# Recurrence gates: the middle output's neighbour rows as one 96-row stacked product instead of a 128-row and a 64-row one

## Chip, core and metric

The kernel runs on one core of a Trainium2 chip. The metric is device time in microseconds (us) from one launch; lower is better. Three runs of the kernel before took 801.54, 803.41 and 803.30 us.

## What is computed

Two layers of a streaming-encoder trunk over 256 tokens of 1024 channels. Each layer normalises the tokens, projects them by one wide matrix, and feeds three mixers: a spatial gate (A), an attention with eight heads (B), and a gated recurrence (C). Their gated outputs are projected, summed, projected again, normalised and added to the tokens. The change touches mixer C only. There, 1280 channels are convolved along time, and two gates are computed from the result by block-diagonal matrices:

```python
xb = xc.reshape(B, S, LRU_BLOCKS, LRU_BW)          # 16 blocks of 80 channels
r = sigmoid(einsum('bshi,hij->bshj', xb, w_a) + b_a)
i = sigmoid(einsum('bshi,hij->bshj', xb, w_x) + b_x)
log_a = -LRU_C * r * softplus(-lam)
h_t = exp(log_a) * h_{t-1} + sqrt(max(1 - exp(2 * log_a), 0)) * (i * xc)
```

A block has 80 channels, a tile of the machine 128 rows: five tiles hold eight blocks, and some blocks lie across two tiles.

## The kernel before

**Weights.** All weights come from main memory as float32 in chunks of up to 128x2048. A chunk is loaded into one of three `raw` buffers by the SP queue, and split into two float32r parts, one rounded (`hi`, written by ScalarE, ACT) and one that holds what the rounding lost (`lo`, written by VectorE, DVE), in one of three pairs `whi`/`wlo`. A product is three matmuls: hi by hi, hi by lo, lo by hi (`mm3`, lines 307 to 309). When a step has used its chunk, `fin` gives the pair back, and `pump` splits the next chunk into it and starts the load after that. So ACT and DVE run ahead of TensorE (PE) by up to three chunks.

**Order.** The table `ORDER` sets one fixed order of steps in each layer. Every engine works its own instructions in that order, and waits on semaphores where it needs another engine. The steps that matter here are `stack` (`conv_stack`, once for each of two groups of five tiles), `la` and `lx` (`lru_gate`, the two gates, each once for each group). Around them the order is: `ga` 0, `la` 0, `lx` 0, `r1` 0, `stack` 1, `pa` 0, `ga` 1, `pa` 1, `la` 1, `r2` 0, `r3` 0, `ga` 2, `pa` 2, `zb` 0, `ga` 3, `zb` 1, `lx` 1.

**The gate matrices.** Of a group's five output tiles, 1 and 3 take their own tile and two neighbours by two full products of three matmuls each. The outputs 0, 2 and 4 take their own tile by three matmuls, and a few rows of their odd neighbours, which are stacked in one operand `xs`. For outputs 0 and 4 that is one run of 32 rows, laid three times one under the other (hi, lo, hi) against weights laid as (hi, hi, lo): one 96-row matmul does all three passes. Output 2 has two neighbours, and so two runs of 32 rows. Two copies fill 128 rows (hi and lo against hi and hi), and the third pass is a matmul of its own over 64 rows (line 930, from `xs[:64]` and `wlo`):

```python
r = 3 * SH if n < 2 else P
mm3(pm, wh[:, e], wl[:, e], xh[:, m], xl[:, m], True, False)
mm(pm, wh[:r, d], xs[:r, n], start=False, stop=n < 2)
if n == 2:
    mm(pm, wl[: 2 * SH, d], xs[: 2 * SH, n], start=False, stop=True)
```

There are eight calls of `lru_gate` (two gates, two groups, two layers), so there are eight such 64-row matmuls.

**Setting up the rows.** `conv_stack` copies the runs into `xs`; the table `SE` names the engine of each ("G" is GpSimd, POOL; "A" is ACT; "V" is DVE). For the stack of output 2, part 0 goes to POOL, and parts 1 and 2 to ACT; before, part 2 does not exist. `split` lays out the weights: line 259 rounds all 1280 columns, lines 261 and 262 copy the stacked columns to lower rows, lines 263 and 264 form the lo part.

Of the kernel before, what the change touches and what calls it, by code (L numbers as in the profile page):

```python
# [13 lines left out]
P = 128  # L14
# [19 lines left out]
# Rows of the per-layer table of channel vectors, 128 channels each.  # L34
R_Q, R_KV, R_LG, R_LB, R_CW, R_CB, R_BA, R_BX, R_LAM, R_N = 0, 3, 5, 13, 21, 61, 71, 81, 91, 101

# A group of five 128-channel tiles holds eight 80-channel blocks, of which the blocks 1, 3, 4 and 6 lie
# across two tiles. The even input tiles meet all outputs in one strip of columns: their own tile's, and
# between them those of the tiles 1 and 3, which two even tiles share (the lower rows from the one, the
# upper rows from the other). The odd input tiles meet their own output, and a few rows of them those of  # L40
# the tiles 0, 2 and 4: those rows stand in one operand for two or three of the float32r products.
COL_EVEN, COL_ODD, COL_STACK, LRU_N = 0, GT * P, (GT + 2) * P, (GT + 5) * P
# Of a stack: the output, its rows, and their runs of 32: input tile, first row.
STACKS = ((0, 32, ((1, 0),)), (4, 32, ((3, 96),)), (2, 64, ((1, 96), (3, 0))))
# [4 lines left out]
# Order of a layer's steps between the ranks and the output projection.  # L49
# [14 lines left out]
# Of what steps the weights make room for the next ones only after the step's arithmetic, and how late.  # L64
LATE = {"ga": 1, "gb": 1, "lx": 1, "pa": 1, "ukv": 1, "uq": 3, "v": 1, "xc": 1}

# Engines that set out the rows of the stacks.
# [7 lines left out]
class Chunk:  # L75
    """A piece of weights on its way: loaded as float32, then split into two float32r parts."""
# [17 lines left out]
def tile_trunk(ctx: ExitStack, tc, I, out):  # L94
# [24 lines left out]
    def ring(pool, s, n, shape, dt=F32):  # L119
        """n buffers taken in turn."""  # L120
        bufs = [pool.tile(shape, dt, tag=f"{s}{i}", name=f"{s}{i}") for i in range(n)]
        turn = [0]

        def take(_=None):
            turn[0] += 1
            return bufs[(turn[0] - 1) % n]

        return take
# [64 lines left out]
    def load(c, parts=1, mid=None):  # L193
        n = c.kt * c.cols
        c.raw = raw_()
        if c.lru is None:
            raw, src, m = v2(c.raw[:, :n], c.cols), c.src(), c.kt // parts
            for i in range(parts):
                nc.sync.dma_start(raw[:, i * m : (i + 1) * m], src[:, i * m : (i + 1) * m])
                if i == 0 and mid:  # L200
                    mid()
            return
        name, l, g = c.lru
        G.memset(c.raw[:, :n], 0.0)

        def piece(row, col, r0, c0, nr, ncol):
            """A piece of a block of the group, its rows and columns counted from the group's start."""
            b = r0 // BW
            nc.sync.dma_start(
                c.raw[row : row + nr, col : col + ncol],  # L210
                I[name][l, g * 8 + b, r0 - b * BW : r0 - b * BW + nr, c0 - b * BW : c0 - b * BW + ncol],
            )

        for b in range(8):
            for k in range(GT):
                r0, r1 = max(b * BW, k * P), min(b * BW + BW, k * P + P)
                if r0 < r1 and k % 2 == 0:
                    piece(r0 - k * P, COL_EVEN + b * BW, r0, b * BW, r1 - r0, BW)
                elif r0 < r1:
                    c0, c1 = max(b * BW, k * P), min(b * BW + BW, k * P + P)  # L220
                    piece(r0 - k * P, COL_ODD + k // 2 * P + c0 - k * P, r0, c0, r1 - r0, c1 - c0)
        for n_, (m, _, runs) in enumerate(STACKS):
            for i, (k, r) in enumerate(runs):
                for b in range(8):
                    r0, r1 = max(b * BW, k * P + r), min(b * BW + BW, k * P + r + SH)
                    c0, c1 = max(b * BW, m * P), min(b * BW + BW, m * P + P)
                    if r0 < r1 and c0 < c1:
                        piece(i * SH + r0 - k * P - r, COL_STACK + n_ * P + c0 - m * P, r0, c0, r1 - r0, c1 - c0)

    def split(c, parts=1, mid=None):  # L230
# [17 lines left out]
        if c.kind == "heads":  # L248
            # Columns of two heads, set out as their unrotated parts and then their rotated ones.
            raw = c.raw[:, :n].rearrange("p (k h r) -> p k h r", h=2, r=HN + HR)  # L250
            for a, b, o in ((0, HN, 0), (HN, HN + HR, 2 * HN)):
                w = b - a
                src = raw[:, :, :, a:b]
                h4, l4 = (v[:, :, o : o + 2 * w].rearrange("p k (h r) -> p k h r", r=w) for v in (c.hi, c.lo))
                act(h4, src, AF.Copy)
                V.tensor_tensor(l4, src, f(h4), ALU.subtract)
            return
        if c.lru:
            act(hi[:, :n], c.raw[:, :n], AF.Copy)
            one, two = slice(COL_STACK, COL_STACK + 2 * P), slice(COL_STACK + 2 * P, n)  # L260
            act(hi[SH : 2 * SH, one], c.raw[:SH, one], AF.Copy)
            act(hi[2 * SH :, two], c.raw[: 2 * SH, two], AF.Copy)
            V.tensor_tensor(lo[:, :n], c.raw[:, :n], f(hi[:, :n]), ALU.subtract)
            V.tensor_tensor(hi[2 * SH : 3 * SH, one], c.raw[:SH, one], f(hi[:SH, one]), ALU.subtract)
            return
# [12 lines left out]
    def pump(most=3, **how):  # L278
        """Splits the next chunks, as far as there is room for their parts, and loads what follows."""
# [76 lines left out]
    def layer_decay(c):  # L356
        # 8 * softplus(-lambda), with log1p(e) = 2 artanh(e / (2 + e)).
# [30 lines left out]
    def sums(n):  # L388
        """Room for n partial means of squares, and the term that goes with them."""
        ss = small("ssq", n + 1)  # L390
        G.memset(ss[:, n : n + 1], EPS)
        return ss
# [33 lines left out]
    def tok_mm(ps, c, t):  # L426
        """Tokens of tile t on partitions, the chunk's channels along the free axis."""
        for k in range(KT):
            lh, ll = hT[0][:, t, k], hT[1][:, t, k]
            rh, rl = c.h(k, 0, CW), c.l(k, 0, CW)  # L430
            mm(ps, lh, rh, start=k == 0, stop=False)  # L431
            mm(ps, lh, rl, start=False, stop=False)  # L432
            mm(ps, ll, rh, start=False, stop=k == KT - 1)  # L433

    def ch_mm(ps, c, seq=None):
        """Two tiles of channels on partitions, all tokens along the free axis."""
# [18 lines left out]
    # ======================================================================  # L455
    with tc.manual_schedule():
# [19 lines left out]
        # The tensor engine reaches its full clock only when it has been busy for some time.  # L476
# [6 lines left out]
        def first_norm(t):  # L483
            """The first layer's norm and transpose: the tokens' factors by a product with a diagonal."""
# [46 lines left out]
        for l in range(L):  # L531
# [169 lines left out]
            def conv_stack(g):  # L701
                """What the odd outputs take from two even tiles, and the stacks of the even outputs."""
# [5 lines left out]
                for n, (_, nr, runs) in enumerate(STACKS):  # L708
                    for p, src in enumerate((xh, xl, xh)[: P // nr]):
                        for i, (k, r) in enumerate(runs):  # L710
                            at = p * nr + i * SH
                            copy(SE.get(("thin", n, p), "V"), xs[at : at + SH, n], f(src[r : r + SH, k]))
# [61 lines left out]
            def attend(i):  # L774
                """The i-th pair of heads' scores, and what follows for the pairs before."""
# [103 lines left out]
            def gated(key, src, n):  # L879
                """Adds a gated projection's channels to the sum."""  # L880
# [24 lines left out]
            hs, gates = {}, {}  # L905

            def lru_gate(key, row):
                def step(g):
# [4 lines left out]
                    for m0 in range(0, GT, 2):  # L913
                        ms = range(m0, min(m0 + 2, GT))
                        ps = bank() if len(ms) == 2 else aux()
                        for m in ms:
# [6 lines left out]
                            else:  # L923
                                n = (0, 4, 2).index(m)
                                d = slice(COL_STACK + n * P, COL_STACK + n * P + P)
                                r = 3 * SH if n < 2 else P
                                mm3(pm, wh[:, e], wl[:, e], xh[:, m], xl[:, m], True, False)
                                mm(pm, wh[:r, d], xs[:r, n], start=False, stop=n < 2)
                                if n == 2:
                                    mm(pm, wl[: 2 * SH, d], xs[: 2 * SH, n], start=False, stop=True)  # L930
# [20 lines left out]
            def recur2(g):  # L951
                # 1 - a^2 = tanh(-log a) (1 + a^2)
# [163 lines left out]
```

## Time and profile before

| | us |
|---|---|
| runs | 801.54, 803.41, 803.30; median 803.3 |
| span of the profiled execution, first to last instruction | 799.7 |
| PE busy, share of the span | 790.8, 99% |
| DVE busy | 551.3, 69% |
| ACT busy | 468.1, 59% |
| POOL busy | 68.9, 9% |

The profile gives the profiled execution's own time as its span only: 799.7 us. The median of the runs lies 3.6 us above it, which is what stands around the span (and what differs between executions). "PE" is the matmul side of TensorE, "PEld" its weight loads. A timeline row gives the start, the duration, the engine, the line in the code, the operation, output<-inputs, and the shape. A matmul's duration (0.28 us) is longer than the distance to the next one, since matmuls overlap in a pipeline; what one costs a full stream is the distance between two starts. Under 800 us, 0.3% is 2.4 us.

### The profile page before, as it was taken

The page shows a single profiled execution, that of the slowest core. Times are in us where ns is not written, and L with a number is a line of the kernel's source. Part 1 is how long each engine was busy: PE and PEld are TensorE (multiplying, and loading weights), DVE is VectorE, ACT ScalarE, POOL GpSimd, SP SyncE. Part 2 cuts the span into 40 slices and gives each one's busy share as a digit, 9 for nine tenths or more (in the row PEclk, how much of TensorE's full clock was granted, in tenths as well). Part 3 has the DMA queues.
Part 4 walks back from the last instruction along what each step waited for, and adds up shares of the span by engine and source line. Part 5 has one row for each costly group of instructions (what it writes and reads, how often), then busy time and mean ns, then how long its engine had stood idle before and what let it go on. Part 6 is the DMA issues. An engine that isn't in the chain of part 4 may idle for free.

```text
span 799.7 us, 15378 instructions
## 1 busy us (share of the span) xinstructions
PE 790.8 (99%) x6453; PEld 780.9 (98%) x6453; DVE 551.3 (69%) x712; ACT 468.1 (59%) x689; POOL 68.9 (9%) x110
## 2 busy tenths in 40 slices
PE   8999999999999999999999999999999999999996
PEld 8999999999999999999999999999999999999996
DVE  5686788567776787555666868776578578775562
ACT  5785766349755736343567776754695574544441
POOL 1100503103000000000010032031210000000000
PEclk9999999999999999999999999999999999999999
DMA  7855454344566465566357626541575656564531
GB/s 235 284 167 183 151 164 131 114 136 151 170 212 211 158 214 170 197 213 216 106 171 242 212 86 210 158 144 34 167 222 161 212 163 207 185 210 149 195 132 53
DMA packets 134205, 137.87 MB, mean 172 GB/s; under 512 B 11046, under 2 KB 130808, under 8 KB 134136
## 3 DMA queue, kind: packets, MB, share of 16 engines
q1 hardware_dynamic: 134120, 136.90, 54.1%
q8 instruction: 50, 0.82, 0.4%
q14 instruction: 19, 0.16, 0.1%
q10 hardware_dynamic: 16, 0.00, 0.0%
HBM read 135.83 MB, written 1.05 MB: 171 GB/s over the span
## 4 chain that ended last, share of the span: by engine, by line
PE 96%; issue 1%; DMA 1%; DVE 0%; ACT 0%; SPq 0%; POOL 0%; POOLq 0%; DVEq 0%
PE mm L307 25%; PE mm L308 25%; PE mm L309 24%; PE mm L431 2%; PE mm L432 2%; PE mm L433 2%; PE mm L549 1%; PE mm L547 1%; PE mm L548 1%; PE aux L843 1%; PE aux L770 1%; PE mm L730 1%; PE mm L731 1%; DMA X<-in_x_dram 1%; PE aux L1024 1%
## 5 line engine op out<-in xcount | busy, mean ns | idle before, releaser
L269 DVE TENSOR_TENSOR wlo<-raw,whi 128x2048 fp32r<-128x2048 f32 (+5 forms) x123 | 264.7, 2157 | 117.0 <-ACT whi L268 116.6
L307 PE MATMUL mm<-hT,whi 128*128 128x256 f32 x1088 | 307.4, 283 | 0.0
L309 PE MATMUL mm<-hT,wlo 128*128 128x256 f32 x1088 | 306.0, 281 | 0.0
L308 PE MATMUL mm<-hT,whi 128*128 128x256 f32 x1088 | 305.9, 281 | 0.0
L268 ACT ACTIVATE whi<-raw 128x2048 fp32r<-128x2048 f32 (+5 forms) x123 | 220.9, 1802 | 68.8 <-PE mm L308 27.8
L308 PEld LDWEIGHTS mm<-hT,whi 128*128 128x128 f32 x1088 | 205.3, 189 | 0.0
L309 PEld LDWEIGHTS mm<-hT,wlo 128*128 128x128 f32 x1088 | 205.2, 189 | 0.1
L307 PEld LDWEIGHTS mm<-hT,whi 128*128 128x128 f32 x1088 | 205.2, 189 | 0.0
L976 ACT ACTIVATE t<-mm 128x512 f32<-128x512 f32 x18 | 10.8, 598 | 53.4 <-PE mm L309 53.4
L397 POOL TENSOR_TENSOR rstd<-rstd,mhalf 128x1 f32<-128x1 f32 x8 | 4.4, 549 | 392.9 <-DVE rstd L396 392.9
L308 PE MATMUL mm<-yc,whi 128*128 128x256 f32 x128 | 36.1, 282 | 0.0
L308 PE MATMUL mm<-ya,whi 128*128 128x256 f32 x128 | 36.1, 282 | 0.0
L307 PE MATMUL mm<-ya,whi 128*128 128x256 f32 x128 | 36.0, 281 | 0.0
L307 PE MATMUL mm<-yc,whi 128*128 128x256 f32 x128 | 36.0, 281 | 0.0
L431 PE MATMUL mm<-whi,hT 128*128 128x256 f32 x128 | 36.0, 281 | 0.0
L309 PE MATMUL mm<-ya,wlo 128*128 128x256 f32 x128 | 35.9, 281 | 0.0
L308 PE MATMUL mm<-yb,whi 128*128 128x256 f32 x128 | 35.9, 281 | 0.0
L309 PE MATMUL mm<-yc,wlo 128*128 128x256 f32 x128 | 35.9, 280 | 0.0
L309 PE MATMUL mm<-yb,wlo 128*128 128x256 f32 x128 | 35.8, 280 | 0.0
L307 PE MATMUL mm<-yb,whi 128*128 128x256 f32 x128 | 35.8, 280 | 0.0
L432 PE MATMUL mm<-wlo,hT 128*128 128x256 f32 x128 | 35.8, 280 | 0.0
L433 PE MATMUL mm<-whi,hT 128*128 128x256 f32 x128 | 35.7, 279 | 0.0
(281 smaller groups left out, 1666.4 us busy)
## 6 DMA issues: line engine op xcount, KB each, us to landing
raw<-in_w_in_dram SPq DMA_DIRECT2D x76, 1024.0 KB
raw<-in_w_proj_a_dram SPq DMA_DIRECT2D x8, 1024.0 KB
raw<-in_w_proj_b_dram SPq DMA_DIRECT2D x8, 1024.0 KB
raw<-in_w_proj_c_dram SPq DMA_DIRECT2D x8, 1024.0 KB
raw<-in_w_out_dram SPq DMA_DIRECT2D x8, 1024.0 KB
raw<-in_mla_w_uq_dram SPq DMA_DIRECT2D x8, 576.0 KB
raw<-in_mla_w_ukv_dram SPq DMA_DIRECT2D x4, 1024.0 KB
raw<-in_w_in_dram SPq DMA_DIRECT2D x4, 640.0 KB
```

The costliest lines, as they stand in the source:

```text
L268: act(hi[:, w], c.raw[:, w], AF.Copy)
L269: V.tensor_tensor(lo[:, w], c.raw[:, w], f(hi[:, w]), ALU.subtract)
L307: mm(ps, lh, rh, start=start, stop=False)
L308: mm(ps, lh, rl, start=False, stop=False)
L309: mm(ps, ll, rh, start=False, stop=stop)
L431: mm(ps, lh, rh, start=k == 0, stop=False)
L432: mm(ps, lh, rl, start=False, stop=False)
L433: mm(ps, ll, rh, start=False, stop=k == KT - 1)
L547: mm(ps, lh, rh, start=j % 2 + k == 0, stop=False)
L548: mm(ps, lh, rl, start=False, stop=False)
L549: mm(ps, ll, rh, start=False, stop=j % 2 * 4 + k == KT - 1)
L976: act(sg, ps, AF.Sigmoid)
```

## The change

The two runs of output 2 overlap in need only by 16 rows each: of tile 1 the rows 112 to 127, of tile 3 the rows 0 to 15. After, both stand in one run of 32: 32 rows of tile 1 from row 96 are copied first, and then 16 rows of tile 3 over the first 16 of them. So output 2 has the same shape as outputs 0 and 4: three parts of 32 rows, one 96-row matmul, and no 64-row one. The copies become 32 and 16 rows for each of three parts, where they were 32 and 32 for each of two. The weights' split treats all three stacks alike: one copy of 32x384 on ACT in place of 32x256 and 64x128, and a lo part of 896 columns in place of 1280. The number of DMAs does not change.

```diff
-STACKS = ((0, 32, ((1, 0),)), (4, 32, ((3, 96),)), (2, 64, ((1, 96), (3, 0))))
+STACKS = ((0, ((1, 0, 32),)), (4, ((3, 96, 32),)), (2, ((1, 96, 32), (3, 0, 16))))
...
-                    r0, r1 = max(b * BW, k * P + r), min(b * BW + BW, k * P + r + SH)
+                    r0, r1 = max(b * BW, k * P + r), min(b * BW + BW, k * P + r + nr)
...
-                        piece(i * SH + r0 - k * P - r, COL_STACK + n_ * P + c0 - m * P, r0, c0, r1 - r0, c1 - c0)
+                        piece(r0 - k * P - r, COL_STACK + n_ * P + c0 - m * P, r0, c0, r1 - r0, c1 - c0)
...
             act(hi[:, :n], c.raw[:, :n], AF.Copy)
-            one, two = slice(COL_STACK, COL_STACK + 2 * P), slice(COL_STACK + 2 * P, n)
-            act(hi[SH : 2 * SH, one], c.raw[:SH, one], AF.Copy)
-            act(hi[2 * SH :, two], c.raw[: 2 * SH, two], AF.Copy)
-            V.tensor_tensor(lo[:, :n], c.raw[:, :n], f(hi[:, :n]), ALU.subtract)
-            V.tensor_tensor(hi[2 * SH : 3 * SH, one], c.raw[:SH, one], f(hi[:SH, one]), ALU.subtract)
+            st = slice(COL_STACK, n)
+            act(hi[SH : 2 * SH, st], c.raw[:SH, st], AF.Copy)
+            V.tensor_tensor(lo[:, :COL_STACK], c.raw[:, :COL_STACK], f(hi[:, :COL_STACK]), ALU.subtract)
+            V.tensor_tensor(hi[2 * SH : 3 * SH, st], c.raw[:SH, st], f(hi[:SH, st]), ALU.subtract)
...
-                for n, (_, nr, runs) in enumerate(STACKS):
-                    for p, src in enumerate((xh, xl, xh)[: P // nr]):
-                        for i, (k, r) in enumerate(runs):
-                            at = p * nr + i * SH
-                            copy(SE.get(("thin", n, p), "V"), xs[at : at + SH, n], f(src[r : r + SH, k]))
+                for n, (_, runs) in enumerate(STACKS):
+                    for p, src in enumerate((xh, xl, xh)):
+                        at = p * SH
+                        for k, r, nr in runs:
+                            copy(SE.get(("thin", n, p), "V"), xs[at : at + nr, n], f(src[r : r + nr, k]))
...
-                                r = 3 * SH if n < 2 else P
                                 mm3(pm, wh[:, e], wl[:, e], xh[:, m], xl[:, m], True, False)
-                                mm(pm, wh[:r, d], xs[:r, n], start=False, stop=n < 2)
-                                if n == 2:
-                                    mm(pm, wl[: 2 * SH, d], xs[: 2 * SH, n], start=False, stop=True)
+                                mm(pm, wh[: 3 * SH, d], xs[: 3 * SH, n], start=False, stop=True)
```

On PE the place is output 2 in the first `la` of a layer (`mm_85` is its accumulator, `xs` the stacked rows, `whi_94` and `wlo_95` the two parts of the gate's weights; a row begins with the line in the code):

```order
 L308 MATMUL mm_85<-xl_1407,whi_94 128x256
 L309 MATMUL mm_85<-xh_1406,wlo_95 128x256
-L928 MATMUL mm_85<-xs_1469,whi_94 128x256
-L930 MATMUL mm_85<-xs_1469,wlo_95 128x256
+L927 MATMUL mm_85<-xs_1469,whi_94 128x256
 L307 MATMUL mm_85<-xh_1406,whi_94 128x256
 L308 MATMUL mm_85<-xl_1407,whi_94 128x256
```

One matmul is gone; those on both sides stand as they stood (the shape in such a row is the output's). The same is so at the seven other places.

On ACT the place is `stack` 1 and the split of `la` 1's weights behind it. Before:

```order
L945 ACT_TABLE_LOAD
L945 ACTIVATE a_2081<-la_2013,sA_777 128x256 x5
L947 ACTIVATE la_2013<-la_2013,sT_776 128x256 x5
L447 ACTIVATE xs_2095<-xl_1255 32x256 x4
L259 ACTIVATE whi_92<-raw_89 128x1280
L261 ACTIVATE whi_92<-raw_89 32x256
L262 ACTIVATE whi_92<-raw_89 64x128
L268 ACTIVATE whi_94<-raw_90 128x2048
```

And after:

```order
L942 ACT_TABLE_LOAD
L942 ACTIVATE a_2079<-la_2013,sA_777 128x256 x5
L944 ACTIVATE la_2013<-la_2013,sT_776 128x256 x5
L447 ACTIVATE xs_2093<-xl_1255 32x256 x3
L447 ACTIVATE xs_2093<-xl_1255 16x256
L447 ACTIVATE xs_2093<-xh_1254 32x256
L447 ACTIVATE xs_2093<-xh_1254 16x256
L260 ACTIVATE whi_92<-raw_89 128x1280
L262 ACTIVATE whi_92<-raw_89 32x384
L268 ACTIVATE whi_94<-raw_90 128x2048
```

ACT has two copies more in front of the gate's weights, and one copy less within them. Each 16-row copy writes over rows that the copy ahead of it has written, and waits for that on its own engine. On DVE and POOL the number of instructions stays the same.

## Rows read from the trace of the kernel before

**Rows 1.** The page, part 1 (busy us, share of the span, instructions) and part 4 (the chain of work that ended last, by engine).
```profile
PE 790.8 (99%) x6453; PEld 780.9 (98%) x6453; DVE 551.3 (69%) x712; ACT 468.1 (59%) x689; POOL 68.9 (9%) x110
...
PE 96%; issue 1%; DMA 1%; DVE 0%; ACT 0%; SPq 0%; POOL 0%; POOLq 0%; DVEq 0%
```

**Rows 2.** Timeline of PE at the first of the eight places: the end of output 2 and the start of output 3, in `la` 0 of layer 0. First column: start in us from the span's start.
```profile
179.92 0.28 PE L309 MATMUL mm<-xh,wlo 128*128 128x256 f32 x1
180.04 0.28 PE L928 MATMUL mm<-xs,whi 128*128 128x256 f32 x1
180.25 0.38 PE L930 MATMUL mm<-xs,wlo 64*128 64x256 f32 x1
180.56 0.39 PE L307 MATMUL mm<-xh,whi 128*128 128x256 f32 x1
180.78 0.28 PE L308 MATMUL mm<-xl,whi 128*128 128x256 f32 x1
180.90 0.28 PE L309 MATMUL mm<-xh,wlo 128*128 128x256 f32 x1
```

**Rows 3.** Timeline of PE at the last of the eight places, in `lx` 1 of layer 1.
```profile
626.85 0.28 PE L928 MATMUL mm<-xs,whi 128*128 128x256 f32 x1
...
627.59 0.28 PE L308 MATMUL mm<-xl,whi 128*128 128x256 f32 x1
```

**Rows 4.** Timeline of PEld, the weight loads, at the first place.
```profile
179.93 0.19 PEld L928 LDWEIGHTS mm<-xs,whi 128*128 128x128 f32 x1
180.25 0.18 PEld L930 LDWEIGHTS mm<-xs,wlo 64*128 64x128 f32 x1
180.56 0.19 PEld L307 LDWEIGHTS mm<-xh,whi 128*128 128x128 f32 x1
180.67 0.19 PEld L308 LDWEIGHTS mm<-xl,whi 128*128 128x128 f32 x1
```

**Rows 5.** Timeline of PE at a 96-row product, the end of output 4 in `la` 0 and the start of `lx` 0.
```profile
181.73 0.29 PE L928 MATMUL aux<-xs,whi 96*128 96x256 f32 x1
181.85 0.28 PE L307 MATMUL mm<-xh,whi 128*128 128x256 f32 x1
181.97 0.28 PE L308 MATMUL mm<-xl,whi 128*128 128x256 f32 x1
```

**Rows 6.** Instructions of the lines 928 and 930: count, duration in ns (least, median, most), first and last start in us, shapes.
```profile
L928 PE MATMUL mm<-xs,whi x16: 276/280/286, 178.8 to 626.8; 96*128 96x256 f32 x8, 128*128 128x256 f32 x8
...
L928 PE MATMUL aux<-xs,whi x8: 281/284/286, 181.7 to 628.5; 96*128 96x256 f32 x8
...
L930 PE MATMUL mm<-xs,wlo x8: 379/381/382, 180.2 to 627.1; 64*128 64x256 f32 x8
```

**Rows 7.** Busy time of ACT from the eviction after `ga` 0 to the end of the split of `la` 1's weights, layer 0 (stretch in us, its length, busy us and count).
```profile
180.40:197.44 17.04, 16.88 (x32) 1.00 0.40 118
```

**Rows 8.** Timeline of ACT in the same part of layer 0. In brackets: idle time before the row, and what ended it.
```profile
178.58 1.92 ACT L268 ACTIVATE whi<-raw 128x2048 fp32r<-128x2048 f32 x1 [2.23 <-PE mm L308]
...
193.66 1.70 ACT L447 ACTIVATE xs<-xl 32x256 fp32r<-32x256 f32 x4
195.38 1.28 ACT L259 ACTIVATE whi<-raw 128x1280 fp32r<-128x1280 f32 x1
196.69 0.42 ACT L261 ACTIVATE whi<-raw 32x256 fp32r<-32x256 f32 x1
197.13 0.31 ACT L262 ACTIVATE whi<-raw 64x128 fp32r<-64x128 f32 x1
```

**Rows 9.** Timeline of DVE, layer 0: the lo parts of the weights of `pa` 0, of `la` 1 (two rows), and of `ga` 3 and `zb` 1 (merged).
```profile
180.53 2.29 DVE L269 TENSOR_TENSOR wlo<-raw,whi 128x2048 fp32r<-128x2048 f32 x1 [2.27 <-ACT whi L268]
...
197.53 1.49 DVE L263 TENSOR_TENSOR wlo<-raw,whi 128x1280 fp32r<-128x1280 f32 x1 [2.14 <-issue]
199.06 0.42 DVE L264 TENSOR_TENSOR whi<-raw,whi 32x256 fp32r<-32x256 f32 x1
...
218.35 4.47 DVE L269 TENSOR_TENSOR wlo<-raw,whi 128x2048 fp32r<-128x2048 f32 x2
```

**Rows 10.** Timeline of PE: first use of the lo part by `pa` 0 (line 309), first use of the stacked rows by `la` 1 (line 928), first use of the lo part by `ga` 3 (line 309).
```profile
185.46 0.28 PE L309 MATMUL mm<-ya,wlo 128*128 128x256 f32 x1
...
202.60 0.28 PE L928 MATMUL mm<-xs,whi 96*128 96x256 f32 x1
...
222.86 0.28 PE L309 MATMUL mm<-hT,wlo 128*128 128x256 f32 x1
```

**Rows 11.** Timeline of ACT around `stack` 0 in layer 0: its four copies, and the first later row that waits for another engine.
```profile
128.29 1.70 ACT L447 ACTIVATE xs<-xl 32x256 fp32r<-32x256 f32 x4
...
134.07 0.60 ACT L847 ACTIVATE t<-mm 128x512 f32<-128x512 f32 x1 [1.40 <-PE mm L309]
```

**Rows 12.** Instructions that write `xs` in 32-row copies, on POOL and on ACT: count, duration in ns (least, median, most), first and last start in us.
```profile
L449 POOL CAST xs<-xh x24: 386/493/2360, 129.7 to 579.9; 32x256 fp32r<-32x256 f32 x24
L447 ACT ACTIVATE xs<-xl x16: 413/416/418, 128.3 to 586.2; 32x256 fp32r<-32x256 f32 x16
```

More of the change, by code (lines that the diff above doesn't have):

```diff
@@ L221, in load @@
                     piece(r0 - k * P, COL_ODD + k // 2 * P + c0 - k * P, r0, c0, r1 - r0, c1 - c0)
-        for n_, (m, _, runs) in enumerate(STACKS):
-            for i, (k, r) in enumerate(runs):
+        for n_, (m, runs) in enumerate(STACKS):
+            for k, r, nr in runs:
                 for b in range(8):
-                    r0, r1 = max(b * BW, k * P + r), min(b * BW + BW, k * P + r + SH)
+                    r0, r1 = max(b * BW, k * P + r), min(b * BW + BW, k * P + r + nr)
                     c0, c1 = max(b * BW, m * P), min(b * BW + BW, m * P + P)
                     if r0 < r1 and c0 < c1:
-                        piece(i * SH + r0 - k * P - r, COL_STACK + n_ * P + c0 - m * P, r0, c0, r1 - r0, c1 - c0)
+                        piece(r0 - k * P - r, COL_STACK + n_ * P + c0 - m * P, r0, c0, r1 - r0, c1 - c0)
     def split(c, parts=1, mid=None):
@@ L707, in conv_stack @@
                     copy(SE.get("wide2", "A"), dst[64:], f(src[64:, 0:3:2]))
-                for n, (_, nr, runs) in enumerate(STACKS):
-                    for p, src in enumerate((xh, xl, xh)[: P // nr]):
-                        for i, (k, r) in enumerate(runs):
-                            at = p * nr + i * SH
-                            copy(SE.get(("thin", n, p), "V"), xs[at : at + SH, n], f(src[r : r + SH, k]))
+                for n, (_, runs) in enumerate(STACKS):
+                    for p, src in enumerate((xh, xl, xh)):
+                        at = p * SH
+                        for k, r, nr in runs:
+                            copy(SE.get(("thin", n, p), "V"), xs[at : at + nr, n], f(src[r : r + nr, k]))
                 cv[g] += (xs, two)
```

## The prediction

> **What bounds the kernel now.** I read the page first: TensorE is busy for 99% of the span, and 96% of the chain that ended last is TensorE [rows 1]. VectorE and ScalarE stand at 69% and 59%. So time that TensorE spends less is time off the end, as long as its operands come early enough. I then read the timeline of TensorE at the place that the change edits. There the reader is to look at the distances between starts, not at the durations. In a run of full products a start follows the one before by 0.12 us, as at 179.92 and 180.04. At the 64-row product this breaks: it starts 0.21 us after the product ahead, the next one 0.31 us later, and the one behind that another 0.22 us later [rows 2]. The weight loads show why. A load normally starts some 0.1 us ahead of its own matmul (179.93 against 180.04), while the matmul before is still running; those of the 64-row product and of the full product behind it start only together with their matmuls, at 180.25 and 180.56 [rows 2, 4]. So here TensorE waits for its own pipe, twice, and no other engine is named as the cause. Last I read ScalarE and VectorE around the same steps, since they get more work.
>
> **TensorE: what goes.** From the start of the 128-row stacked product to the start of the second product behind the 64-row one, 0.74 us pass (180.04 to 180.78) [rows 2]; at the last of the eight places it is 0.74 as well (626.85 to 627.59) [rows 3]. There are eight such places, one for each 64-row product [rows 6]. After the change two products stand in that stretch, a 96-row one and a full one. What this costs is in the trace: output 4 ends with just such a 96-row product, and its start and the next two lie 0.12 and 0.12 us apart [rows 5]. There are sixteen of these now, eight on each of two kinds of bank [rows 6]. So the stretch becomes 0.24 us long, and each place gives 0.74 - 0.24 = 0.50 us. Eight places: **-4.0 us**.
>
> The bounds. Downwards, the least that leaving out a product can give is its own slot in the stream: 8 x 0.12 = 0.96 us. Upwards, reading one product further (180.04 to 180.90, three slots of 0.12 in its place) gives 0.86 - 0.36 = 0.50 again, so the stall is over by then and 4.0 is also the top. I take the top, because the 96-row product that takes the place is not an estimate: it stands in the trace in the same chain of products, with the same neighbours.
>
> **ScalarE: what comes.** At each `stack`, six copies in place of four. Four take 1.72 us from the first start to the next instruction (193.66 to 195.38), 0.43 each, and the duration hardly varies (413 to 418 ns) [rows 8, 12]. No row has a 16-row copy on this engine; I take 0.42 for it, since in the split a 64x128 copy takes 0.31 and a 32x256 one 0.42 [rows 8], so it is the columns that are paid for, and those stay 256. The two own-engine waits are priced by line 261, which must wait for line 259 and starts 0.03 us after that ends [rows 8]. Together +0.9 us. In the split behind it, one copy of 32x384 replaces two that take 0.75 us (196.69 to 197.44). From 0.42 at 256 columns and 1.28 at 1280, a column costs 0.84 ns, so 384 take 0.53: -0.2 us. Net, `la` 1's rounded weights come **0.7 us later**.
>
> **VectorE and GpSimd.** The lo part shrinks from 1280 columns (1.49 us) to 896; from 2.29 at 2048 a column costs 1.04 ns, so 1.09 us. The second piece grows from 0.42 to 0.55 [rows 9]. That is 0.27 us less each time. It may also start sooner, as it no longer reads what the last ScalarE copy writes; I do not count on it. GpSimd keeps its six copies of 256 columns. All this lies beside TensorE, and is worth nothing by itself.
>
> **Who is late next.** I looked for the operand whose lead over TensorE is smallest behind the place, and moved both sides. ScalarE works without a pause from 180.40 to 197.44 (16.88 us of 17.04) [rows 7], starting behind a split that waits for TensorE's step before `la` 0 [rows 8]; so it does not come earlier when TensorE does.
> - `pa` 0: its lo part is ready at 180.53 + 2.29 = 182.82 and first used at 185.46 [rows 9, 10], 2.6 us of lead. `la` 0 and `lx` 0 ahead of it lose 0.5 us each, so 1.6 are left.
> - `la` 1: the last piece is ready at 199.48 and used at 202.60 [rows 9, 10], 3.1 us of lead. TensorE comes 1.0 us earlier; the piece comes 0.7 - 0.27 = 0.4 later. 1.7 are left.
> - `ga` 3: half of 4.47 us behind 218.35 is 220.6, used at 222.86 [rows 9, 10]: 2.3 us of lead. TensorE is 1.5 us earlier by then, and if nothing else moves 0.8 are left.
> - `stack` 0 has 0.9 us more of copies in front of an eviction for which ScalarE now idles 1.40 us [rows 11].
>
> So every lead shrinks and none is used up, and nothing of the 4.0 us is given back. If that cover were gone, each microsecond that `la` 1's weights come later than 1.7 us would cost two, one in each layer.
>
> **The sum.** The profiled span is 799.7 us, and 799.7 - 4.0 = 795.7. The median of the runs lies 3.6 us above the span, and I keep that: 803.3 - 4.0 = **799.3 us**, or -0.50%. A measurement of this kernel can tell about 0.3% from no change, which is 2.4 us.
>
> **Rivals.**
>
> *Only the slot is saved.* The stall belongs to the place and not to the 64 rows (to the change from one output to the next, say), and a product with fewer rows costs what a full one does. Then only 8 x 0.12 = 0.96 us go: 802.3 us, no change that can be told. For it: both late starts lie around a change of output. Against it: output 4 ends in the same way on a 96-row product, followed by another output on another bank, without a late start [rows 5], and only the 64-row matmul and the one behind it have their loads late [rows 4]. The Trainium skill has a rule for this side: "TensorE: Matmul & The Clock Gate", in the table of "Why this matters for your kernels", says that a product over 32 rows takes the time of one over 128, which would make the 64-row one worth one slot. The same skill in "TensorEngine Tiling (Array Packing)", "Key Properties", says that a change of the tiling mode drains the engine, and lists 64 rows as a mode of its own; by that each 64-row product among full ones pays for two changes. The two late starts in the trace, 0.31 and 0.21 us at this one product, agree with the second page.
>
> *The copies stall ScalarE.* This is the way to a slower kernel. The last three copies of `stack` 1 are new or changed, and two wait on their own engine. If each of these three took what the slowest 32-row copy takes on GpSimd, 2.36 us [rows 12], in place of one at 0.42, ScalarE would be 6.7 us later, less 0.2 in the split. `la` 1's lead of 3.1 us, less the 1.0 by which TensorE comes earlier, covers 2.1; TensorE would wait 4.4 us in each layer, and the kernel end at 803.3 - 4.0 + 8.8 = 808.1 us. It turns slower from about 4 us of delay on ScalarE. Against it: sixteen copies on this engine within 5 ns of each other [rows 12].
>
> *The leads are used up in part.* A load from memory or a split that keeps its old time makes TensorE wait at `ga` 3 or behind it. With half of the gain given back: 801.3 us, no change that can be told. Against it: 0.8 us is the least lead left, by the count that moves nothing else forward.
>
> **How the numbers follow.** Forecast 0.85; only the slot 0.08; leads used up in part 0.04; copies stall 0.03. The first is faster by more than 0.3%, the next two within it, the last slower: 0.85, 0.12, 0.03. The runs before spread over 1.9 us (801.54 to 803.41), with two of three at the top, so the median after may well lie 2 us below the sum, at 797.3, with nothing changed in the mechanism. Upwards I go as far as the gain half given back, 801.3. The case of the slot alone and the stall lie outside, with 0.11 between them.
>
> **What would show it.** In the profile after: eight matmuls fewer and no 64-row one; at the end of output 2, starts 0.12 us apart throughout, and each weight load ahead of its matmul again; TensorE busy some 4 us less, and still 99%. On ScalarE six copies of about 0.42 us at each `stack`, and on VectorE pieces of about 1.1 and 0.55 us. If the 96-row product at that place starts late or makes its neighbour start late, the first step is wrong. If the distances are right and the span has not shrunk by some 4 us, TensorE waits somewhere new, and I would look at `pa` 0, `la` 1 and `ga` 3 first.

## The result, and the profile after

| | before | after |
|---|---|---|
| median of the runs, us | 803.36 (801.54 to 803.77, 4 runs) | 798.60 (798.34 to 799.42, 4 runs) |
| ratio, 95% interval | | 0.9948 [0.9934, 0.9963] |
| span of the profiled execution, us | 799.7 | 796.6 |
| first recurrence product to the end of the span, us | 621.2 | 617.2 |

The kernel became faster by 0.5%: by the ratio 4.2 us, where 4.0 were forecast (799.3 us). The profiled spans differ by only 3.1 us. The last row of the table says why. In the kernel before, the first recurrence product (`la` 0 of layer 0, the first place that the change touches on TensorE) starts at 178.50; after, at 179.32. So this execution came 0.8 us later to that place. It was 0.7 us late at 28 us already (one and the same product starts at 28.06 before and at 28.74 after), ahead of everything that the change touches. From the first recurrence product to the end the time is 799.74 - 178.50 = 621.24 before and 796.56 - 179.32 = 617.24 after: 4.0 us less.

The page of the kernel after, parts 1 and 4, answers to [rows 1]:

```profile
PE 788.1 (99%) x6445; PEld 780.2 (98%) x6445; DVE 548.9 (69%) x712; ACT 469.3 (59%) x689; POOL 70.5 (9%) x110
...
PE 94%; DMA 2%; issue 1%; DVE 1%; ACT 1%; SPq 0%; POOL 0%; POOLq 0%; DVEq 0%; ACTq 0%
```

Eight matmuls are gone (6453 to 6445), and TensorE is still busy for 99%. Its busy time fell by 2.7 us and not by the 4 that the prediction named as a sign: from the first recurrence product on it fell by 4.0 (614.7 to 610.7), and ahead of it this execution has 1.3 more. The timeline of TensorE at the first place, the end of output 2, answers to [rows 2], and that of the weight loads to [rows 4]:

```profile
180.75 0.28 PE L309 MATMUL mm<-xh,wlo 128*128 128x256 f32 x1
180.87 0.28 PE L927 MATMUL mm<-xs,whi 96*128 96x256 f32 x1
180.99 0.28 PE L307 MATMUL mm<-xh,whi 128*128 128x256 f32 x1
181.10 0.28 PE L308 MATMUL mm<-xl,whi 128*128 128x256 f32 x1
```

```profile
180.75 0.19 PEld L927 LDWEIGHTS mm<-xs,whi 96*128 96x128 f32 x1
180.87 0.19 PEld L307 LDWEIGHTS mm<-xh,whi 128*128 128x128 f32 x1
180.99 0.19 PEld L308 LDWEIGHTS mm<-xl,whi 128*128 128x128 f32 x1
```

Starts are 0.12 us apart right through, and each load runs ahead of its matmul again (180.75 against 180.87). From the stacked product to the second one behind it are now 0.23 us (180.87 to 181.10), where there were 0.74. The last of the eight places reads the same against [rows 3]:

```profile
624.16 0.28 PE L927 MATMUL mm<-xs,whi 96*128 96x256 f32 x1
624.28 0.28 PE L307 MATMUL mm<-xh,whi 128*128 128x256 f32 x1
624.40 0.28 PE L308 MATMUL mm<-xl,whi 128*128 128x256 f32 x1
```

ScalarE and VectorE in the second `stack` of layer 0 and the split of `la` 1's weights, and the first use of the stacked rows there, answer to [rows 8, 9, 10] (brackets: idle time before the row, and what ended it):

```profile
194.49 1.60 ACT L447 ACTIVATE xs<-xl 32x256 fp32r<-32x256 f32 x4
196.11 0.86 ACT L447 ACTIVATE xs<-xh 32x256 fp32r<-32x256 f32 x2
196.99 1.27 ACT L260 ACTIVATE whi<-raw 128x1280 fp32r<-128x1280 f32 x1
198.29 0.53 ACT L262 ACTIVATE whi<-raw 32x384 fp32r<-32x384 f32 x1
```

```profile
198.30 1.09 DVE L263 TENSOR_TENSOR wlo<-raw,whi 128x896 fp32r<-128x896 f32 x1 [2.08 <-ACT whi L260]
199.42 0.55 DVE L264 TENSOR_TENSOR whi<-raw,whi 32x384 fp32r<-32x384 f32 x1
```

```profile
202.38 0.28 PE L927 MATMUL mm<-xs,whi 96*128 96x256 f32 x1
```

The six copies, merged by their input with the shape of the first, take 2.5 us (194.49 to 196.99) where four took 1.7. VectorE starts behind line 260 and no longer behind the last ScalarE copy. The last piece of the weights is ready at 199.97 and used at 202.38: a lead (the time from an operand being ready to its first use) of 2.4 us, where it was 3.1.

### The profile page after: what moved, and what is told of

Its sections match the earlier page's. It is cut to its first block, busy times and chain, and to the rows that moved or that the text cites. A ratio compares the mean times of both kernels' runs of the same rounds, so it can differ in the third digit from the quotient of the medians.

```text
span 796.6 us, 15355 instructions
## 1 busy us (share of the span) xinstructions
PE 788.1 (99%) x6445; PEld 780.2 (98%) x6445; DVE 548.9 (69%) x712; ACT 469.3 (59%) x689; POOL 70.5 (9%) x110
## 4 chain that ended last, share of the span: by engine, by line
PE 94%; DMA 2%; issue 1%; DVE 1%; ACT 1%; SPq 0%; POOL 0%; POOLq 0%; DVEq 0%; ACTq 0%
PE mm L308 25%; PE mm L307 25%; PE mm L309 25%; PE mm L431 2%; PE mm L433 2%; PE mm L432 2%; DMA raw<-in_w_in_dram 1%; PE aux L843 1%; PE mm L730 1%; PE aux L770 1%; PE mm L731 1%; DMA X<-in_x_dram 1%; PE mm L549 1%; PE aux L1021 1%; PE mm L1020 1%
```

## The experiments

The theory, called the drain theory below: among products over full or nearly full rows, one over 64 rows makes TensorE empty its pipe before and behind it, and that costs 0.50 us at each place, the product's own slot in the stream included. "Drain" is a name for the stall here: the rows show late starts and late weight loads, not the pipe itself. Its rivals: the stall belongs to the place (the slot theory), the 64-row product is slow in itself, or the gain comes from the copies and the smaller split.

The start of the first recurrence product varies by 2 us from one profiled execution to another, with the same work of TensorE ahead of it. So the table gives the time from there to the end of the span beside the ratio. "Difference" is that time against the kernel that the run was made from. It is taken from one profiled execution of each kernel; the kernel before, `mid64` and `copies_alone`, and with them `add64` and `add32`, come to the same time within 0.1 us. The intervals of the ratios are 1.4 to 2.3 us wide, so differences of 1 us or so rest on this column.

| run | made from | ratio to before, 95% | span | first product | to the end | difference |
|---|---|---|---|---|---|---|
| kernel before | | | 799.7 | 178.5 | 621.2 | |
| kernel after | before | 0.9948 [0.9934, 0.9963] | 796.6 | 179.3 | 617.2 | -4.0 |
| rows128 | before | 0.9960 [0.9947, 0.9973] | 797.3 | 179.1 | 618.2 | -3.1 |
| mid64 | before | 1.0000 [0.9991, 1.0009] | 801.8 | 180.6 | 621.2 | 0.0 |
| twice64 | before | 1.0017 [1.0007, 1.0026] | 802.6 | 180.4 | 622.1 | +0.9 |
| add64 | after | 1.0002 [0.9993, 1.0010] | 800.2 | 178.9 | 621.3 | +4.0 |
| add96 | after | 0.9971 [0.9960, 0.9982] | 798.4 | 180.2 | 618.2 | +0.9 |
| add32 | after | 0.9999 [0.9991, 1.0008] | 800.6 | 179.3 | 621.3 | +4.1 |
| copies_alone | before | 1.0003 [0.9994, 1.0012] | 801.8 | 180.5 | 621.3 | 0.0 |
| five_copies | after | 0.9963 [0.9950, 0.9976] | 797.2 | 178.8 | 618.4 | +1.2 |
| seven_copies | after | 0.9983 [0.9974, 0.9992] | 800.2 | 180.0 | 620.3 | +3.0 |
| ten_copies | after | 1.0035 [1.0021, 1.0049] | 803.2 | 179.5 | 623.8 | +6.5 |

### The same number of products, all over 128 rows

```diff
-                                    mm(pm, wl[: 2 * SH, d], xs[: 2 * SH, n], start=False, stop=True)
+                                    mm(pm, wl[:, d], xs[:, n], start=False, stop=True)
```

> The kernel before, with the separate product of output 2 over all 128 rows of the operands in place of 64 (the upper rows then cancel the pass of weight hi by input lo for the neighbours, so that pass is left out of output 2). All else, the copies included, is as before. Drain theory (a change between 64-row and full products stops TensorE's pipe): the eight places shrink from 0.74 us to three slots of 0.12, 0.36 us, so 8 x 0.38 = 3.0 us less than before, ratio 0.996; starts 0.12 us apart throughout. Slot theory (the stall belongs to the place, a product costs one slot whatever its rows): same time as before, ratio 1.000.

Measured: 798.93 us, ratio 0.9960 [0.9947, 0.9973], and 3.1 us less from the first product on. Timeline of TensorE at the first place:

```profile
180.69 0.28 PE L928 MATMUL mm<-xs,whi 128*128 128x256 f32 x1
180.80 0.28 PE L930 MATMUL mm<-xs,wlo 128*128 128x256 f32 x1
180.92 0.28 PE L307 MATMUL mm<-xh,whi 128*128 128x256 f32 x1
181.03 0.28 PE L308 MATMUL mm<-xl,whi 128*128 128x256 f32 x1
```

The product computes over twice the rows and makes the kernel faster. Nothing but the rows of this product differs, at the same place, with the same copies and the same split. The slot theory expected no change, and falls. Three quarters of the gain are the rows; the last quarter, 0.9 us, is the slot of the product that the change leaves out.

### The 64-row product at another place in the output

```diff
-                                mm3(pm, wh[:, e], wl[:, e], xh[:, m], xl[:, m], True, False)
-                                mm(pm, wh[:r, d], xs[:r, n], start=False, stop=n < 2)
-                                if n == 2:
-                                    mm(pm, wl[: 2 * SH, d], xs[: 2 * SH, n], start=False, stop=True)
+                                mm(pm, wh[:, e], xh[:, m], start=True, stop=False)
+                                if n == 2:
+                                    mm(pm, wl[: 2 * SH, d], xs[: 2 * SH, n], start=False, stop=False)
+                                mm(pm, wh[:, e], xl[:, m], start=False, stop=False)
+                                mm(pm, wl[:, e], xh[:, m], start=False, stop=False)
+                                mm(pm, wh[:r, d], xs[:r, n], start=False, stop=True)
```

> The kernel before, with the 64-row product moved from the end of output 2 to behind its first full product; the 128-row stacked product ends the output (same sums in another order). Drain theory: the two late starts move with it into the middle of the output, about 0.50 us over the slots again, and the change to output 3 runs at 0.12 us; same time as before, ratio 1.000. If the stall belongs to the change from one output to the next: the late start stays at the end of output 2, where no 64-row product stands now.

Measured: 803.03 us, ratio 1.0000 [0.9991, 1.0009]. Timeline of TensorE through output 2 and into output 3:

```profile
181.76 0.28 PE L927 MATMUL mm<-xh,whi 128*128 128x256 f32 x1
181.97 0.38 PE L929 MATMUL mm<-xs,wlo 64*128 64x256 f32 x1
182.28 0.39 PE L930 MATMUL mm<-xl,whi 128*128 128x256 f32 x1
182.51 0.28 PE L931 MATMUL mm<-xh,wlo 128*128 128x256 f32 x1
182.62 0.28 PE L932 MATMUL mm<-xs,whi 128*128 128x256 f32 x1
182.74 0.28 PE L307 MATMUL mm<-xh,whi 128*128 128x256 f32 x1
```

The distances of 0.21, 0.31 and 0.23 us went with the 64-row product into the middle of the output. The change to output 3 (182.62 to 182.74) runs at 0.12. So the change from one output to the next has no part in it.

### Two 64-row products in a row

```diff
-                                    mm(pm, wl[: 2 * SH, d], xs[: 2 * SH, n], start=False, stop=True)
+                                    mm(pm, wl[: 2 * SH, d], xs[: 2 * SH, n], start=False, stop=False)
+                                    mm(pm, wl[: 2 * SH, d], xs[: 2 * SH, n], start=False, stop=True)
```

> The kernel before, with the 64-row product twice in a row (its pass is counted twice in output 2). Drain theory: the second one stands in the same mode and costs one slot of about 0.12 us or little more, 8 x 0.12 = 1.0 us more than before, ratio 1.001. If instead each 64-row product is slow by itself (its duration is 0.38 us against 0.28, and its load starts only with it): about 0.31 us more at each place, 2.5 us more than before, ratio 1.003.

Measured: 804.04 us, ratio 1.0017 [1.0007, 1.0026], and 0.9 us more from the first product on. Timeline of TensorE at the first place:

```profile
181.98 0.28 PE L928 MATMUL mm<-xs,whi 128*128 128x256 f32 x1
182.19 0.39 PE L930 MATMUL mm<-xs,wlo 64*128 64x256 f32 x1
182.41 0.28 PE L931 MATMUL mm<-xs,wlo 64*128 64x256 f32 x1
182.62 0.38 PE L307 MATMUL mm<-xh,whi 128*128 128x256 f32 x1
182.84 0.28 PE L308 MATMUL mm<-xl,whi 128*128 128x256 f32 x1
```

The whole stretch is 0.86 us against 0.74 with one: the second product costs 0.12, one slot. The second one also has its weight load ahead of it, while the first and the full product behind them have not. Timeline of the weight loads there:

```profile
182.19 0.18 PEld L930 LDWEIGHTS mm<-xs,wlo 64*128 64x128 f32 x1
182.30 0.19 PEld L931 LDWEIGHTS mm<-xs,wlo 64*128 64x128 f32 x1
182.62 0.19 PEld L307 LDWEIGHTS mm<-xh,whi 128*128 128x128 f32 x1
```

The 64-row product is not slow in itself. What is paid for is going from one kind to the other and back, here once for a group of two; longer groups were not run. The distances are 0.21, 0.22, 0.21 and 0.22 us, where a lone 64-row product has 0.21, 0.31 and 0.22. That fits an estimate of 0.19 us for each of the two changes: 0.09 over the slot on the product behind the change, and 0.10 on the one after that. With a lone product the 0.10 of the first change and the 0.09 of the second fall on the same start. This division is read from the distances; no run tests it by itself.

### 64, 96 or 32 rows put back into the changed kernel

```diff
-                                mm(pm, wh[: 3 * SH, d], xs[: 3 * SH, n], start=False, stop=True)
+                                mm(pm, wh[: 3 * SH, d], xs[: 3 * SH, n], start=False, stop=n < 2)
+                                if n == 2:
+                                    mm(pm, wh[: 2 * SH, d], xs[: 2 * SH, n], start=False, stop=True)
```

The control has `3 * SH` in the last line, the third run `1 * SH`.

> The changed kernel, with a 64-row product put back at the end of output 2 behind the 96-row one (from the rounded weights, so output 2 gets an extra term). Copies and split are those of the changed kernel. Drain theory: 0.50 us more at each of eight places, 4.0 us more than the changed kernel, so within 0.1% of the kernel before, ratio 1.000. Slot theory: 1.0 us more than the changed kernel, ratio 0.996 to before. If the gain came from fewer or other copies and the smaller split: no more than 1 us of it goes.

> The changed kernel, with a second 96-row product at the end of output 2 (output 2 gets its neighbours' rows twice). Both theories: one slot of 0.12 us at each place, 1.0 us more than the changed kernel, ratio to before 0.996. It is the control of the run with 64 rows put back: by the drain theory the two differ by 3.0 us, by the slot theory not at all.

> The changed kernel, with a 32-row product at the end of output 2 behind the 96-row one (output 2 gets an extra term). Drain theory, if any product over fewer rows than the full products and the 96-row ones use is a change of mode: about 4.0 us more than the changed kernel, ratio to before about 1.000. If only 64 rows are special: 1.0 us more, ratio 0.996.

Measured: 803.08 us with 64 rows (ratio 1.0002 [0.9993, 1.0010]), 800.32 with 96 (0.9971 [0.9960, 0.9982]), 802.38 with 32 (0.9999 [0.9991, 1.0008]). From the first product on they take 4.0, 0.9 and 4.1 us more than the changed kernel. With 64 rows put back the whole gain is gone, although the copies, the waits on ScalarE's own writes and the smaller split are those of the changed kernel; so none of these carries any of it. Which part of the weights is read has no say either: this product stalls with the rounded part, and the one over 128 rows above did not with the lo part. The same product over 96 rows costs its slot. Over 32 rows it costs what it costs over 64, as the timeline of that run shows:

```profile
180.82 0.28 PE L927 MATMUL mm<-xs,whi 96*128 96x256 f32 x1
181.03 0.38 PE L929 MATMUL mm<-xs,whi 32*128 32x256 f32 x1
181.34 0.38 PE L307 MATMUL mm<-xh,whi 128*128 128x256 f32 x1
181.56 0.28 PE L308 MATMUL mm<-xl,whi 128*128 128x256 f32 x1
```

### The copies without the product

```diff
+                for _ in range(2):
+                    copy("A", xs[SH : 2 * SH, 0], f(xl[:SH, 1]))
                 cv[g] += (xs, two)
```

> The kernel before, with two more 32-row copies on ScalarE in each stack step (they repeat a copy that is there, so the result is unchanged). TensorE's work is as before. My count: 0.9 us more on ScalarE, covered by leads of 2.3 us and more; same time as before, ratio 1.000 within 0.1%. Rival (copies stall ScalarE): up to 1.8 us more, ratio 1.002.

Measured: 803.21 us, ratio 1.0003 [0.9994, 1.0012]; from the first product on 621.3 us against 621.2. Two more copies of ScalarE in each `stack` cost nothing.

### How many copies it takes

```diff
+                for _ in range(10 * g):
+                    copy("A", xs[SH : 2 * SH, 0], f(xl[:SH, 1]))
                 cv[g] += (xs, two)
```

The other two runs have 5 and 7 in place of 10.

> The changed kernel, with ten more copies on ScalarE in the second group's stack step of each layer (each repeats a copy that is there; the result is unchanged). That is 4.3 to 4.4 us more ahead of the second group's weights. By the trace of the changed kernel the lead there is 2.4 us at the stacked product, and 2.0 us at the step behind it. If the leads are counted rightly, TensorE waits 2.0 to 2.7 us in each layer: 4 to 5.4 us more than the changed kernel, ratio to before 1.000 to 1.002, with the wait at the second group's first gate, seen as late starts there. If ScalarE's work at this place never reaches TensorE: as the changed kernel, ratio 0.995.

> The changed kernel, with five more copies on ScalarE in the second group's stack step of each layer (result unchanged): 2.2 us more, against leads of 2.4 us at the stacked product and 2.0 us at the step behind it in the trace of the changed kernel. If the leads are counted rightly, TensorE waits 0 to 0.3 us in each layer: 0 to 0.6 us more than the changed kernel, ratio to before 0.995 to 0.996, and the granted clock stays at 1.00. If delays on ScalarE reach TensorE in full, whatever the lead: 4.4 us more, ratio 1.000.

> The changed kernel, with seven more copies there (result unchanged): 3.1 us more. By the leads TensorE waits 0.7 us at the stacked product and some 0.4 us behind it: about 1.1 us in each layer, 2.2 us more than the changed kernel, ratio to before 0.9975, if the granted clock stays at 1.00 as the waits are short. If the waits let the clock fall as with ten copies (a stretch of 3.4 us at 0.50, which took 1.7 us more): up to 3.4 us on top, ratio up to 1.002.

Measured: 805.22 us with ten (1.0035 [1.0021, 1.0049]), 799.95 with five (0.9963 [0.9950, 0.9976]), 802.01 with seven (0.9983 [0.9974, 0.9992]). From the first product on they take 6.5, 1.2 and 3.0 us more than the changed kernel, for 4.4, 2.2 and 3.1 us more of ScalarE in each of two layers. So the leads do hide copies up to a point and then TensorE waits. At `la` 1 there is no wait with five: the last piece is ready at 201.68 and the stacked product starts at 201.87. With seven it waits there, as the lead of 2.4 us says. Timeline of TensorE at `la` 1 in the run with seven:

```profile
202.78 0.28 PE L308 MATMUL mm<-xl,whi 128*128 128x256 f32 x1
203.21 0.39 PE L309 MATMUL mm<-xh,wlo 128*128 128x256 f32 x1
203.88 0.35 PE L929 MATMUL mm<-xs,whi 96*128 96x256 f32 x1 [0.29 <-DVE whi L264]
204.07 0.28 PE L307 MATMUL mm<-xh,whi 128*128 128x256 f32 x1
```

But all three came out above what I had expected (0 to 0.6 with five, 2.2 with seven at an unchanged clock, 4 to 5.4 with ten). With five, the part missed is at `ga` 3. I had counted only the two steps next to the copies, `la` 1 and `ga` 2, and the prediction itself names a third. Timeline of TensorE there, in the run with five:

```profile
221.86 0.28 PE L308 MATMUL mm<-hT,whi 128*128 128x256 f32 x1
222.17 0.39 PE L309 MATMUL mm<-hT,wlo 128*128 128x256 f32 x1
222.39 0.28 PE L307 MATMUL mm<-hT,whi 128*128 128x256 f32 x1
```

It starts its lo product 0.31 us behind the one before, and the next one 0.22 later: 0.3 us over two slots, and a like one at `ga` 2 (204.52 to 205.08, 0.56 for two slots). Twice 0.6 us makes the 1.2. With seven, each layer lost 0.9 us at `la` 1, where 0.7 were expected, and again 0.3 at `ga` 2 and 0.3 at `ga` 3, at a granted clock of 1.00. With ten, a second thing comes in. Windows of TensorE in the run with ten, layer 0 (stretch, length, busy us and count, granted clock, share and rate of the DMAs):

```profile
204.00:205.00 1.00, 0.68 (x3) 0.97 0.00 0
205.00:208.00 3.00, 3.00 (x16) 0.50 0.67 186
208.00:209.00 1.00, 1.00 (x9) 0.82 1.09 383
209.00:212.00 3.00, 3.00 (x28) 1.00 1.06 345
```

Between 202.0 and 204.7 TensorE stood still three times, waiting for pieces of the weights. Then the granted clock is 0.50, which is 1.2 GHz, until 208.4: 16 products in 3 us where 28 run in the same time at 1.00. In layer 1 of the same execution, with waits at the same place, it stayed at 1.00:

```profile
595.00:602.00 7.00, 5.51 (x40) 1.00 0.47 136
```

Counted from the first product of `la` 0 to the first of `gb` 0 and set against the same stretch of the changed kernel, layer 1 lost 59.67 - 56.89 = 2.8 us by waits alone, and layer 0 60.58 - 56.81 = 3.8 us by waits and clock.

## Why the prediction was right

**TensorE bounds the kernel, so its time comes off the end.** Held. 4.0 us went from its stream, and 4.0 from the end, counted from the first recurrence product. Set side by side product by product from there on, the two traces differ by 0.49 to 0.50 us at each of the eight places, and no other distance between two starts changes by 0.05 us. The granted clock around the places is 1.00 in both, so it has no part in the gain.

**0.74 us at each place become 0.24.** Held: 0.23 to 0.24 at the first and the last place. The 4.0 are made of 3.1 for the change of rows (`rows128`) and 0.9 for the slot (4.0 less 3.1; 0.9 again in `add96`). Both bounds that the prediction set are so accounted for: the lower one, 0.96, is the slot alone, and what lies above it is the stall.

**The late weight loads as the sign.** Held, as far as the runs go: wherever a 64- or 32-row product stands among the others, its start and the two behind it are late, and nowhere else in a `lru_gate` without waits for operands. In the kernel before, 24 starts there lie 0.2 us or more behind the one ahead, three at each 64-row product, and all others under 0.14; in the kernel after, in `rows128` and in `add96` no start is late. By the Trainium skill, "TensorEngine Tiling (Array Packing)", "Key Properties", a change of the tiling mode drains the engine; the same page's "Available Configurations" lists tilings of 64 and of 32 rows beside those of 128. The runs agree as far as they go, and put a price on it: 0.38 us beside the slot for the change there and back (0.74 less 0.36), in a stream of products at 0.12, and nothing for 96 rows. They do not show whether a change between 64 and 32 rows has a price, nor where between 64 and 96 rows it ends. That TensorE "waits for its own pipe", as the prediction has it, is an inference from the late loads: by the profile's ends, which are modelled, the product ahead still runs for 0.07 us when the 64-row one starts (180.04 + 0.28 against 180.25). The Trainium skill's rule in "TensorE: Matmul & The Clock Gate" ("Why this matters for your kernels"), that 32 rows take the time of 128, fits the second of two 64-row products, which took one slot. For a lone one among full products, over 64 rows or 32, the runs differ from it, 0.50 us against 0.12.

**ScalarE 0.7 us later, VectorE 0.27 us less.** The new pieces took 0.53, 1.09 and 0.55 us as worked out. The six copies took 2.5 us, +0.8, where 0.9 were expected, and the 16-row ones cost what 32-row ones cost (414 to 418 ns). Net, ScalarE's last piece for `la` 1 came 0.56 us later, counted from `la` 0 (197.44 - 178.50 = 18.94 before, 198.82 - 179.32 = 19.50 after). The lead of `la` 1 fell from 3.1 to 2.4 us and not to 1.7: the possibility that I left out of the count, that VectorE no longer waits for the last ScalarE copy, is what happened. Against the time at which each kernel reached `la` 0, the last piece came 0.3 us earlier (199.48 - 178.50 = 20.98 before, 199.97 - 179.32 = 20.65 after).

**No lead is used up.** Held. The lead of `pa` 0 became 1.6 us, as counted (ready at 183.64, used at 185.25), and ScalarE still idles 0.62 us behind `stack` 0. The lead of `ga` 3 was forecast at 0.8 if nothing else moved; in the trace after it is 1.7, since ScalarE and VectorE, counted from `la` 0, came 1.0 us earlier there along with TensorE:

```profile
218.17 4.46 DVE L269 TENSOR_TENSOR wlo<-raw,whi 128x2048 fp32r<-128x2048 f32 x2
```

```profile
222.15 0.28 PE L309 MATMUL mm<-hT,wlo 128*128 128x256 f32 x1
```

Half of 4.46 behind 218.17 is 220.4. The list of steps had a gap: `ga` 2, with 2.0 us of lead after, is not on it, and with five more copies (2.2 us of ScalarE) TensorE lost 0.3 us at `ga` 2 and 0.3 at `ga` 3, and none at `la` 1. Fewer than five were not run on the changed kernel.

**The sum against the median.** Here the result is right and one reading was not. I took the 3.6 us between the profiled span and the median as what lies around a span. In the profiled executions of the runs here, the time stands 1.7 to 1.8 us above its span (798.34 and 796.6; 805.03 and 803.2). By that, the profiled execution of the kernel before took 799.7 + 1.8 = 801.5 us, the lowest of its runs (801.54), and the rest of the 3.6 is how its executions differ. Since I kept the difference and moved the sum, it cancelled. The forecast of 799.3 us lies 0.7 above the median of 798.6, within that spread.

## What to carry to other kernels

In a dense stream of matmuls, read the distance between starts and not the durations; a single product over few rows among full ones may cost several slots (here 0.50 us, four of them), and filling its rows up to the shape of its neighbours was cheaper here than keeping it small. If small products can't be avoided, put them next to each other: here the price was paid once for two. When work is moved onto a helper engine, count the lead of every operand behind that place until it has recovered, not only of the next one.

## What I had not expected

- 32 rows cost the same as 64 (0.50 us at each place with the slot that it adds, +4.1 us in all).
- The time at which an execution comes to its first recurrence product, 178.5 to 180.6 us, is spread over 2 us, half of what the change brings. Part of it can be seen in the profile after: the first recurrence input waits for its weights there. Timeline of TensorE:

```profile
28.13 0.28 PE L308 MATMUL mm<-hT,whi 128*128 128x256 f32 x1
28.74 0.38 PE L309 MATMUL mm<-hT,wlo 128*128 128x256 f32 x1 [0.32 <-DVE wlo L269]
```

  These are 0.61 us for a slot of 0.12; before, the same two starts lie 0.14 apart (27.92 to 28.06). Ahead of it, ScalarE's split behind a load from memory starts at 24.44 after and at 23.76 before. What makes the early loads later in one execution than in another stays open.
- A delay on ScalarE can cost more than the part of it that the lead leaves open. With ten copies that part is 4.4 - 2.4 = 2.0 us in a layer. Layer 1 lost 2.8 us, 0.6 of it at the two steps behind; layer 0 lost 3.8, as the waits there were followed by 3.4 us at a granted clock of 0.50. Why the clock fell in only one of the two stays open.
